# An encoder block on one core: modulation sums ordered one per attention unit, and a later place for the weight chunk's load

## The chip, the cores and the metric

The kernel runs on one core of a Trainium2 chip. The metric is the device time of one launch in microseconds (us). The time before is 1429.08 us, the median of three runs (1422.79 to 1430.99).

## The reference

One layer of an encoder block for one sequence of 1024 tokens with 1024 features, all in float32:

```python
mod = silu(c) @ w_ada + b_ada                    # 6 vectors of 1024
sh_m, sc_m, gt_m, sh_f, sc_f, gt_f = split(mod)
h = rms_norm(x, g_mix) * (1 + sc_m) + sh_m
qa, ka, va, qb, kb, vb = split(h @ w_in)
o_a = neighbourhood_attention(qa, ka, va, rpb)   # 8 heads of 64, an 8 x 16 window
o_b = differential_attention(qb, kb, vb)         # 4 heads, two maps of 64, values of 128
o_b = rms_norm(o_b, subln_w) * (1 - lambda_init)
x = x + gt_m * (concat(o_a, o_b) @ w_out)
h = rms_norm(x, g_ffn) * (1 + sc_f) + sh_f
gate, up = split(h @ w_gate_up)
x = x + gt_f * ((silu(gate) * up) @ w_down)
return rms_norm(x, g_final)
```

A differential head subtracts a multiple of one softmax map from the other. The change touches how four of the six vectors of `mod` are summed (`gt_m`, `sh_f`, `sc_f`, `gt_f`), and when the columns of `w_in` are loaded.

## The kernel before, in words

**Precision.** TensorE multiplies in the type fp32r. Each float32 operand is split into a high part (a copy in fp32r, made by ScalarE) and a low part (the rest, made by VectorE or GpSimd), and each product is three matmuls: high x high, high x low, low x high. So nearly every result that goes back to TensorE gives ScalarE one copy and VectorE one subtraction. In the names, a trailing `h` and `l` are the two parts: `w_h` and `w_l` of a chunk of `w_in`, `pth` and `ptl` (neighbourhood) or `ath` and `atl` (differential) of the transposed probabilities, `vsh` and `vsl` of values. TensorE's lines are all that of a helper, L89, so its rows are told apart by tiles.

**Stages.** From 0 to 66 us the kernel loads `x`, normalizes it and makes the first two modulation vectors. From 66 to 640 us it runs the attention, to 714 us the output projection and the second norm, and to 1421 us the FFN.

**The attention.** A list `seq` has 64 units: 32 of neighbourhood attention, `Na(pr, i)`, four pairs of heads by eight blocks of 128 queries, and then 32 of differential attention, `Da(h, i)`. A unit goes through these steps:
- `score()`: its score matmuls (`ns` and `s` for the two kinds), into two banks for the two heads or maps, alternately; then on VectorE the addition of bias or distance with the row minimum (`np<-ns`, L784; `p<-s`, L682; the minimum is in `nst` or `st`), and on ScalarE the exponential.
- `trans()`: VectorE normalizes (L801 and L803) or combines the two maps (L694 to L697), TensorE transposes (`nt`, `at`), ScalarE copies the high part and VectorE subtracts the low part (L814, L705). These low parts are the last instructions of `trans()`.
- `pv()`, for every second unit: the products with the values, and their addition (`on`, L838 and L839).

The main loop works on the units in a staggered way: in the round of unit n it issues `score()` of n + 1, `pv()` of n - 1, `norm()` of n - 2, `finish()` of n - 3, one step of the modulation sums, and `trans()` of n:

```python
        fill(step * share[1])
        next(mods, None)
...
        u.trans(ats)
```

Between these, `fill()` takes matmuls from a queue of fillers, which give TensorE work while a softmax runs: `gen_qk` (L475) makes the queries or keys of a head from a chunk of `w_in`, in two halves of 24 matmuls (`hf` 0 and 1, tiles `nq`, `nk`, `q`, `k`), `gen_v` (L496) makes values from two chunks in four parts (`ip` 0 to 3, tiles `v0p` to `v3p`), and `gen_mo` makes parts of the output projection (`mo`).

**The chunks of `w_in`.** `next_w()` takes the next chunk, of 128 x 1024, and splits what is still unsplit in the list `loading`; `load_next()` splits what is in `loading` and issues the load of a further chunk (`w_r`, L226) on SyncE's queue. The split is a copy by ScalarE (`w_h`, L201) and a subtraction by GpSimd (`w_l`, L202). One chunk is loaded ahead.

**The modulation sums.** `gen_mods` (L578 to L616) makes a vector `silu(c) @ w` as eight steps for each half of 512 columns: a load of a tile `wm` of 128 x 512 (L587, on GpSimd's queue, up to three under way), and on VectorE `acc = wm * silc[j] + acc` (L596 for the first of the eight, L600 for the others). There are three vectors, so 48 steps, one in each round of the main loop. A further load is issued behind each step. There is a single `acc` tile. After the eighth step the half is finished: for the gate vector, ScalarE and VectorE split `acc` (`gh` L607, `gl` L608), a bias row is loaded (`gb`, L611, SyncE's queue), TensorE adds over the partitions (`gt`) and VectorE adds the bias (`gate_m`, L616); for the others TensorE makes columns (`mvp`) and VectorE adds (`AB`, L210 and L212). A fourth vector, the FFN's gate, is made by the same function in the first group of the FFN, with its loads on SyncE's queue; there the first step of each half is ordered behind an instruction of the second norm, `late_t["done"]`.

**The order.** The program text is not the order of execution. A scheduler sorts the instructions of each engine by a simulated time and the dependencies, and engines then run their own lists strictly in order, waiting for one another by semaphores. `PE.after(x, y)` (L76) adds an order without a wait: `x` stands behind `y` in the schedule. A sum depends only on its `wm` tile and on `acc`, so the scheduler may put it ahead of the round in whose text it stands.

Of the kernel before, what the change touches and what calls it, by code (L numbers as in the profile page):

```python
# [10 lines left out]
F32 = mybir.dt.float32  # L11
# [4 lines left out]
ALU = mybir.AluOpType  # L16
# [3 lines left out]
P = 128  # L20
# [84 lines left out]
def block_kernel(ctx: ExitStack, tc: tile.TileContext, t: dict):  # L105
# [368 lines left out]

    def gen_qk(kind, key, name):  # L475
        w_h, w_l = next_w()
        load_next()
        hd = key[1] + (4 if key[0][0] == "n" else 0)
        slot = qk_t(hd, 0 if kind == "q" else 2)
        mark = G.memset(slot[:, 0:1].bitcast(F32), 0.0)  # L480
        for hf in range(2):
            out = bank(f"{name}_{hf}")
            for k in range(KT):
                sl = slice(k * P, (k + 1) * P)
                hi, lo = hh[k // 2][:, k % 2, :], hl[k // 2][:, k % 2, :]
                for ti, (w, h) in enumerate([(w_h, hi), (w_h, lo), (w_l, hi)]):
                    mm = PE.matmul(out, w[:, sl], h[:, hf * 512:(hf + 1) * 512],
                                   start=(k == 0 and ti == 0), stop=(k == KT - 1 and ti == 2))
                    if mark is not None:
                        PE.after(mm, mark)  # L490
                        mark = None
                yield 0.65
            made = evac_q(out, hd, hf) if kind == "q" else evac_k(out, hd, hf)
        qkv[key] = made

    def gen_v(n, evac):  # L496
        ws = [next_w(), next_w()]
        load_next()
        for ip in range(4):
            out = bank(f"v{n}p{ip}")  # L500
            for ii in range(2):
                i = 2 * ip + ii
                for k in range(KT):
                    w_h, w_l = ws[k // 4]
                    sl = slice((k % 4) * 256, (k % 4 + 1) * 256)
                    hi = hh[k // 2][:, k % 2, i * P:(i + 1) * P]
                    lo = hl[k // 2][:, k % 2, i * P:(i + 1) * P]
                    for ti, (h, w) in enumerate([(hi, w_h), (lo, w_h), (hi, w_l)]):
                        PE.matmul(out[:, ii * 256:(ii + 1) * 256], h, w[:, sl],
                                  start=(k == 0 and ti == 0), stop=(k == KT - 1 and ti == 2))  # L510
                    if k % 2:
                        yield 0.65
            evac(n, ip, out)
        qkv["vd", n] = True

    def v_tiles(n):
# [58 lines left out]
            tb.append(tbh)  # L575
        qkv["tb", pr] = tb

    def gen_mods(steps, raw_of, acc_of, tmp_of, gate, queue, first=None, ahead=2):  # L578

        steps = [(which, n, j) for which in steps for n in range(2) for j in range(KT)]  # L580
        raws = []
# [9 lines left out]
        for at, (which, n, j) in enumerate(steps):  # L591
            load()
            yield
            if j == 0:
                acc = acc_of(f"acc{which}{n}")
                head = V.tensor_scalar(out=acc, in0=raws[at], scalar1=silc[:, 0:1], scalar2=None, op0=ALU.mult)  # L596
                if first is not None:
                    PE.after(head, first)
            else:
                V.scalar_tensor_tensor(out=acc, in0=raws[at], scalar=silc[:, j:j + 1], in1=acc, op0=ALU.mult, op1=ALU.add)  # L600
            if j < KT - 1:
                continue
            if which in (3, 4):
# [14 lines left out]
    queue = []  # L618
# [38 lines left out]
    class Da:  # L657
# [30 lines left out]
        def trans(self, ats):  # L688
# [9 lines left out]
            for b in range(2):  # L698
                tps = bank(f"at{h}_{i}_{b}")
                for j in range(4):  # L700
                    PE.transpose(tps[:, j * P:(j + 1) * P], p[0][:, (4 * b + j) * P:(4 * b + j + 1) * P], ident)
                src = tps.rearrange("p (a b) -> p a b", a=4)
                hi, lo = at_h[b][:, :, e * P:(e + 1) * P], at_l[b][:, :, e * P:(e + 1) * P]
                A.activation(out=hi, in_=src, func=AF.Copy)
                V.tensor_tensor(out=lo, in0=src, in1=hi.bitcast(F32), op=ALU.subtract)  # L705

        def pv(self, ats, pvs):
            h, i = self.h, self.i
# [56 lines left out]
    class Na:  # L765
# [24 lines left out]
        def trans(self, ats):  # L790
# [19 lines left out]
            for m in range(2):  # L810
                src = tps[:, m * 512:m * 512 + nk].rearrange("p (a b) -> p a b", b=P)
                dsl = (slice(None), slice(sl, sl + nk // P), slice(e * P, (e + 1) * P))
                A.activation(out=pt_h[m][dsl], in_=src, func=AF.Copy)
                V.tensor_tensor(out=pt_l[m][dsl], in0=src, in1=pt_h[m][dsl].bitcast(F32), op=ALU.subtract)  # L814

        def pv(self, ats, pvs):
            pr, i = self.pr, self.i
# [49 lines left out]
    def gate_m():  # L867
        if 2 not in gates:
# [1 line left out]
        return gates[2]  # L870

    mods = gen_mods((2, 3, 4), mraw_t, lambda nm: mp.tile([P, 512], F32, tag="acc", bufs=1, name=nm),
                    lambda nm, dt=F32: mp.tile([P, 512], dt, tag="sq", bufs=4, name=nm), gate_m, G)

    oh, ol, wo, x1, late_t = [], [], [[], []], [], {}

    o_at = {}

# [222 lines left out]
    for gi, fs in enumerate(groups):  # L1101
# [27 lines left out]
        if gi == 0:  # L1129
            gtf = gate_t("gate_f")  # L1130
            for _ in gen_mods((5,), lambda nm: lp.tile([P, 512], F32, tag="dt", bufs=4, name=nm),
                              lambda nm: lp.tile([P, 512], F32, tag="macc", bufs=1, name=nm),
                              lambda nm, dt=F32: lp.tile([P, 512], dt, tag="sil", bufs=3, name=nm), lambda: gtf, SY, late_t["done"]):
                pass
        wd = []
        for f in fs:
# [82 lines left out]
```

## Time and profile before

| | us |
|---|---|
| median of three runs | 1429.08 |
| lowest and highest | 1422.79, 1430.99 |
| the profiled execution | 1423.15 |
| its span | 1421.4 |
| TensorE (PE) busy in the span | 1378.5 (97%) |
| VectorE (DVE) busy | 724.2 (51%) |
| ScalarE (ACT) busy | 461.9 (32%) |
| GpSimd (POOL) busy | 291.5 (21%) |

The profile is of one execution; the span is what the trace covers of its time. Busy times are per engine and overlap. SP is the queue of SyncE, which issues most DMAs. The granted clock, PEclk, is the mean TensorE clock of a stretch, where 1.00 is the higher of two levels (2.4 GHz) and 0.50 the lower (1.2 GHz). A busy time of TensorE is modelled from the records of its matmuls, so a long one at the lower clock is busy too.

### The profile page before, as it was taken

The page shows a single profiled execution, that of the slowest core. Times are in us where ns is not written, and L with a number is a line of the kernel's source. Part 1 is how long each engine was busy: PE and PEld are TensorE (multiplying, and loading weights), DVE is VectorE, ACT ScalarE, POOL GpSimd, SP SyncE. Part 2 cuts the span into 40 slices and gives each one's busy share as a digit, 9 for nine tenths or more (in the row PEclk, how much of TensorE's full clock was granted, in tenths as well). Part 3 has the DMA queues.
Part 4 walks back from the last instruction along what each step waited for, and adds up shares of the span by engine and source line. Part 5 has one row for each costly group of instructions (what it writes and reads, how often), then busy time and mean ns, then how long its engine had stood idle before and what let it go on. Part 6 is the DMA issues. An engine that isn't in the chain of part 4 may idle for free.

```text
span 1421.4 us, 17696 instructions
## 1 busy us (share of the span) xinstructions
PE 1378.5 (97%) x7033; PEld 1142.2 (80%) x7033; DVE 724.2 (51%) x1324; ACT 461.9 (32%) x817; POOL 291.5 (21%) x318
## 2 busy tenths in 40 slices
PE   5899998999999999999999999999999999999997
PEld 5698787887898777787888888888888888888886
DVE  5775766748777589656747215113411421151136
ACT  5544444545445365423531220221121012202212
POOL 3021322311112000001430320421221132204201
PEclk8999999999999998999999999999999999999999
DMA  9231514433021251023321210211111121102102
GB/s 371 105 119 49 189 61 129 134 101 114 24 89 60 82 199 53 8 68 112 119 76 43 75 59 1 89 45 45 31 73 45 31 62 57 55 6 89 45 22 96
DMA packets 43826, 114.82 MB, mean 81 GB/s; under 512 B 12723, under 2 KB 12979, under 8 KB 42464
## 3 DMA queue, kind: packets, MB, share of 16 engines
q1 hardware_dynamic: 39280, 99.37, 20.8%
q0 software_dynamic: 4464, 14.33, 3.1%
q8 instruction: 55, 0.90, 0.3%
q14 instruction: 27, 0.22, 0.0%
HBM read 99.26 MB, written 14.42 MB: 80 GB/s over the span
## 4 chain that ended last, share of the span: by engine, by line
PE 90%; DVE 4%; ACT 2%; DMA 1%; issue 1%; POOL 1%; POOLq 0%; DVEq 0%; ACTq 0%
PE gu L89 33%; PE dn L89 17%; PE s L89 5%; PE pv L89 3%; PE mo L89 3%; PE k L89 3%; PE q L89 3%; PE mp L89 3%; PE at L89 2%; PE nk L89 2%; PE npv L89 2%; PE v1p L89 2%; PE v2p L89 2%; PE nq L89 1%; PE v3p L89 1%
## 5 line engine op out<-in xcount | busy, mean ns | idle before, releaser
L1126 DVE TENSOR_TENSOR sg<-sg,gu 128x512 f32<-128x512 f32 x44 | 30.2, 687 | 352.0 <-ACT sg L1125 352.0
L89 PE MATMUL dn<-wd_h,al 128*128 128x512 f32 x352 | 136.9, 389 | 0.0
L89 PE MATMUL dn<-wd_l,ah 128*128 128x512 f32 x352 | 136.9, 389 | 0.0
L89 PE MATMUL dn<-wd_h,ah 128*128 128x512 f32 x352 | 136.9, 389 | 0.0
L1156 DVE TENSOR_TENSOR dt<-dn,gate_f 128x512 f32<-128x512 f32 x96 | 66.4, 691 | 88.1 <-PE dn L89 88.1
L202 POOL TENSOR_TENSOR wg_l<-wg_r,wg_h 128x1024 fp32r<-128x1024 f32 x20 | 48.4, 2420 | 271.9 <-ACT wg_h L201 271.9
L684 ACT ACTIVATE p<-p,st 128x1024 f32<-128x1024 f32 x64 | 73.5, 1148 | 61.7 <-DVE st L682 58.7
L201 ACT ACTIVATE wg_h<-wg_r 128x1024 fp32r<-128x1024 f32 x22 | 23.3, 1060 | 212.2 <-PE dn L89 154.2
L89 PE MATMUL s<-qk 64*128 64x512 f32 x384 | 88.6, 425 | 2.9 <-DVE st L682 2.9
L682 DVE CUSTOM_DVE_ANT_0 p<-s,dist 128x1024 f32<-128x1024 f32 x64 | 77.1, 1218 | 23.7 <-PE s L89 22.8
L202 POOL TENSOR_TENSOR wd_l<-wd_r,wd_h 128x1024 fp32r<-128x1024 f32 x20 | 48.0, 2400 | 163.7 <-ACT wd_h L201 163.7
L89 PEld LDWEIGHTS dn<-wd_h,ah 128*128 128x128 f32 x352 | 66.1, 188 | 13.8
L89 PEld LDWEIGHTS dn<-wd_h,al 128*128 128x128 f32 x352 | 66.1, 188 | 13.7
L89 PEld LDWEIGHTS dn<-wd_l,ah 128*128 128x128 f32 x352 | 66.1, 188 | 13.7
L89 PEld LDWEIGHTS s<-qk 64*128 64x128 f32 x384 | 54.3, 189 | 26.0 <-issue 9.0
L1157 DVE TENSOR_TENSOR x<-x,dt 128x512 f32<-128x512 f32 x96 | 70.0, 729 | 2.9
L1125 ACT ACTIVATE sg<-gu 128x512 f32<-128x512 f32 x44 | 26.0, 590 | 138.4 <-PE gu L89 136.6
L89 PE MATMUL gu<-h2h,wg_h 128*128 128x512 f32 x176 | 68.9, 392 | 0.4 <-DVE sg L1126 0.4
L89 PE MATMUL gu<-h2l,wg_h 128*128 128x512 f32 x176 | 68.7, 391 | 0.0
L89 PE MATMUL gu<-h2h,wu_h 128*128 128x512 f32 x176 | 68.6, 390 | 0.0
L89 PE MATMUL gu<-h2l,wu_h 128*128 128x512 f32 x176 | 68.6, 390 | 0.0
L89 PE MATMUL gu<-h2h,wg_l 128*128 128x512 f32 x176 | 68.5, 389 | 0.0
(308 smaller groups left out, 3467.3 us busy)
## 6 DMA issues: line engine op xcount, KB each, us to landing
w_r<-in_w_in_dram SPq DMA_DIRECT2D x24, 512.0 KB, 3.7
wm<-in_w_ada_l_dram POOLq DMA_DIRECT2D x48, 256.0 KB, 3.5
wg_r<-in_w_gate_up_dram SPq DMA_DIRECT2D x22, 512.0 KB, 3.6
wu_r<-in_w_gate_up_dram SPq DMA_DIRECT2D x22, 512.0 KB, 3.5
wd_r<-in_w_down_dram SPq DMA_DIRECT2D x22, 512.0 KB, 3.5
x<-in_x_dram SPq DMA_DIRECT2D x16, 512.0 KB, 8.5
wada<-in_w_ada_s_dram SPq DMA_DIRECT2D x6, 1024.0 KB, 11.8
v<-vd SPq DMA_DIRECT2D x4, 1024.0 KB, 5.7
```

The lines of the kernel that those rows point to most:

```text
L89: ins = call(*args, **kw)
L201: A.activation(out=hi, in_=raw, func=AF.Copy)
L202: lo_engine().tensor_tensor(out=lo, in0=raw, in1=hi.bitcast(F32), op=ALU.subtract)
L682: V.tensor_tensor_reduce(out=pr, in0=s, in1=dists[0][:, d0:d0 + 1024], scale=1.0, scalar=BIG, op0=ALU.add, op1=ALU.min, accum_out=self.st[ ...
L684: A.activation(out=pr, in_=pr, func=AF.Exp, scale=-1.0, bias=self.st[:, m:m + 1], accum_out=self.st[:, 2 + m:3 + m])
L1125: A.activation(out=sg, in_=gu[:, 0:512], func=AF.Silu)
L1126: V.tensor_tensor(out=sg, in0=sg, in1=gu[:, 512:1024], op=ALU.mult)
L1156: V.tensor_tensor(out=dt_, in0=out, in1=gtf[:, dsl], op=ALU.mult)
L1157: V.tensor_tensor(out=x1[i][:, dsl], in0=x1[i][:, dsl], in1=dt_, op=ALU.add)
```

## The change

First, each step of the modulation sums is ordered behind the instruction that `mark()` names, if there is one. In the attention that is the latest low part written by a `trans()` so far, `late_t["low"]`: since the step stands ahead of `trans()` in the text, it is a low part of the unit before. In the FFN it is `late_t["done"]`, now for every step and not only for the first of eight. Second, `load_next()` moves from the start of a chunk to its middle, behind the first half in `gen_qk`, and behind the second of four parts in `gen_v`. Lines behind the first hunk shift by one to four.

```diff
--- before.py
+++ after.py
@@ -474,7 +474,6 @@
 
     def gen_qk(kind, key, name):
         w_h, w_l = next_w()
-        load_next()
         hd = key[1] + (4 if key[0][0] == "n" else 0)
         slot = qk_t(hd, 0 if kind == "q" else 2)
         mark = G.memset(slot[:, 0:1].bitcast(F32), 0.0)
@@ -491,11 +490,12 @@
                         mark = None
                 yield 0.65
             made = evac_q(out, hd, hf) if kind == "q" else evac_k(out, hd, hf)
+            if hf == 0:
+                load_next()
         qkv[key] = made
 
     def gen_v(n, evac):
         ws = [next_w(), next_w()]
-        load_next()
         for ip in range(4):
             out = bank(f"v{n}p{ip}")
             for ii in range(2):
@@ -511,6 +511,8 @@
                     if k % 2:
                         yield 0.65
             evac(n, ip, out)
+            if ip == 1:
+                load_next()
         qkv["vd", n] = True
 
     def v_tiles(n):
@@ -575,7 +577,9 @@
             tb.append(tbh)
         qkv["tb", pr] = tb
 
-    def gen_mods(steps, raw_of, acc_of, tmp_of, gate, queue, first=None, ahead=2):
+    late_t = {}
+
+    def gen_mods(steps, raw_of, acc_of, tmp_of, gate, queue, mark, ahead=2):
 
         steps = [(which, n, j) for which in steps for n in range(2) for j in range(KT)]
         raws = []
@@ -593,11 +597,11 @@
             yield
             if j == 0:
                 acc = acc_of(f"acc{which}{n}")
-                head = V.tensor_scalar(out=acc, in0=raws[at], scalar1=silc[:, 0:1], scalar2=None, op0=ALU.mult)
-                if first is not None:
-                    PE.after(head, first)
+                step = V.tensor_scalar(out=acc, in0=raws[at], scalar1=silc[:, 0:1], scalar2=None, op0=ALU.mult)
             else:
-                V.scalar_tensor_tensor(out=acc, in0=raws[at], scalar=silc[:, j:j + 1], in1=acc, op0=ALU.mult, op1=ALU.add)
+                step = V.scalar_tensor_tensor(out=acc, in0=raws[at], scalar=silc[:, j:j + 1], in1=acc, op0=ALU.mult, op1=ALU.add)
+            if mark() is not None:
+                PE.after(step, mark())
             if j < KT - 1:
                 continue
             if which in (3, 4):
@@ -702,7 +706,7 @@
                 src = tps.rearrange("p (a b) -> p a b", a=4)
                 hi, lo = at_h[b][:, :, e * P:(e + 1) * P], at_l[b][:, :, e * P:(e + 1) * P]
                 A.activation(out=hi, in_=src, func=AF.Copy)
-                V.tensor_tensor(out=lo, in0=src, in1=hi.bitcast(F32), op=ALU.subtract)
+                late_t["low"] = V.tensor_tensor(out=lo, in0=src, in1=hi.bitcast(F32), op=ALU.subtract)
 
         def pv(self, ats, pvs):
             h, i = self.h, self.i
@@ -811,7 +815,7 @@
                 src = tps[:, m * 512:m * 512 + nk].rearrange("p (a b) -> p a b", b=P)
                 dsl = (slice(None), slice(sl, sl + nk // P), slice(e * P, (e + 1) * P))
                 A.activation(out=pt_h[m][dsl], in_=src, func=AF.Copy)
-                V.tensor_tensor(out=pt_l[m][dsl], in0=src, in1=pt_h[m][dsl].bitcast(F32), op=ALU.subtract)
+                late_t["low"] = V.tensor_tensor(out=pt_l[m][dsl], in0=src, in1=pt_h[m][dsl].bitcast(F32), op=ALU.subtract)
 
         def pv(self, ats, pvs):
             pr, i = self.pr, self.i
@@ -870,9 +874,9 @@
         return gates[2]
 
     mods = gen_mods((2, 3, 4), mraw_t, lambda nm: mp.tile([P, 512], F32, tag="acc", bufs=1, name=nm),
-                    lambda nm, dt=F32: mp.tile([P, 512], dt, tag="sq", bufs=4, name=nm), gate_m, G)
-
-    oh, ol, wo, x1, late_t = [], [], [[], []], [], {}
+                    lambda nm, dt=F32: mp.tile([P, 512], dt, tag="sq", bufs=4, name=nm), gate_m, G, lambda: late_t.get("low"))
+
+    oh, ol, wo, x1 = [], [], [[], []], []
 
     o_at = {}
 
@@ -1130,7 +1134,7 @@
             gtf = gate_t("gate_f")
             for _ in gen_mods((5,), lambda nm: lp.tile([P, 512], F32, tag="dt", bufs=4, name=nm),
                               lambda nm: lp.tile([P, 512], F32, tag="macc", bufs=1, name=nm),
-                              lambda nm, dt=F32: lp.tile([P, 512], dt, tag="sil", bufs=3, name=nm), lambda: gtf, SY, late_t["done"]):
+                              lambda nm, dt=F32: lp.tile([P, 512], dt, tag="sil", bufs=3, name=nm), lambda: gtf, SY, lambda: late_t["done"]):
                 pass
         wd = []
         for f in fs:
```

VectorE, neighbourhood attention, second pair of heads (`np_2` is its third unit). Before, from the last `ptl` of unit 0 on:

```order
L814 TENSOR_TENSOR ptl_0_1_1542<-nt_0_1550,pth_0_1_1540 128x2x128
L616 TENSOR_TENSOR gate_m<-gt_1532,gb_1530 128x512
L600 SCALAR_TENSOR_TENSOR acc_1632<-wm_1537,silc,acc_1632 128x512
L600 SCALAR_TENSOR_TENSOR acc_1632<-wm_1634,silc,acc_1632 128x512
L784 ISA np_2_1591,nst_2_1590<-ns_2_1589,tb_1424 128x384
L784 ISA nst_2_1590 128x1
L784 ISA np_2_1591,nst_2_1590<-ns_2_1589,tb_1428 128x384
L784 ISA nst_2_1590 128x1
L600 SCALAR_TENSOR_TENSOR acc_1632<-wm_1709,silc,acc_1632 128x512
```

With the change:

```order
L818 TENSOR_TENSOR ptl_0_1_1542<-nt_0_1550,pth_0_1_1540 128x2x128
L600 TENSOR_SCALAR acc_1630<-wm_1340,silc 128x512
L620 TENSOR_TENSOR gate_m<-gt_1532,gb_1530 128x512
L788 ISA np_2_1591,nst_2_1590<-ns_2_1589,tb_1424 128x384
L788 ISA nst_2_1590 128x1
L788 ISA np_2_1591,nst_2_1590<-ns_2_1589,tb_1428 128x384
L788 ISA nst_2_1590 128x1
L788 ISA np_3_1662,nst_3_1661<-ns_3_1660,tb_1424 128x384
L788 ISA nst_3_1661 128x1
```

The first sum of a new vector (`acc_1632`, now `acc_1630`) is now behind `ptl_0_1`, no other follows, and `np_2` and `np_3` come next.

VectorE at the change to the third pair of heads (`np_0`, `np_1`, with new tables). Before:

```order
L596 TENSOR_SCALAR acc_2183<-wm_1979,silc 128x512
L814 TENSOR_TENSOR ptl_3_0_1983<-nt_7_2033,pth_3_0_1981 128x2x128
L814 TENSOR_TENSOR ptl_3_1_1984<-nt_6_1992,pth_3_1_1982 128x3x128
L600 SCALAR_TENSOR_TENSOR acc_2183<-wm_2028,silc,acc_2183 128x512
L814 TENSOR_TENSOR ptl_3_1_1984<-nt_7_2033,pth_3_1_1982 128x2x128
L616 TENSOR_TENSOR gate_m<-gt_2132,gb_2130 128x512
L600 SCALAR_TENSOR_TENSOR acc_2183<-wm_2136,silc,acc_2183 128x512
L461 SCALAR_TENSOR_TENSOR qk_2009<-nq_1_2074,qk_2009 128x512
L600 SCALAR_TENSOR_TENSOR acc_2183<-wm_2185,silc,acc_2183 128x512
L600 SCALAR_TENSOR_TENSOR acc_2183<-wm_2258,silc,acc_2183 128x512
L784 ISA np_0_2052,nst_0_2051<-ns_0_2050,tb_2042 128x256
L784 ISA nst_0_2051 128x1
```

With the change:

```order
L602 SCALAR_TENSOR_TENSOR acc_1630<-wm_1864,silc,acc_1630 128x512
L818 TENSOR_TENSOR ptl_3_1_1984<-nt_7_2031,pth_3_1_1982 128x2x128
L602 SCALAR_TENSOR_TENSOR acc_1630<-wm_1923,silc,acc_1630 128x512
L461 SCALAR_TENSOR_TENSOR qk_2007<-nq_1_2074,qk_2007 128x512
L788 ISA np_0_2050,nst_0_2049<-ns_0_2048,tb_2040 128x256
L788 ISA nst_0_2049 128x1
L788 ISA np_0_2050,nst_0_2049<-ns_0_2048,tb_2044 128x256
L788 ISA nst_0_2049 128x1
L612 TENSOR_TENSOR gl_2127<-acc_1630,gh_2126 128x512
L788 ISA np_1_2080,nst_1_2079<-ns_1_2078,tb_2040 128x384
L788 ISA nst_1_2079 128x1
```

Here the new vector's sums (`acc_2183`) stood ahead of `np_0`; now the old vector's last ones (`acc_1630`) stand there, and the split of it (`gl`) behind `np_0`. In the order before, two more of the new vector's sums stand between `np_1` and `np_2`; in the order now its first one stands behind `np_2`.

TensorE, differential attention, last head, scores of its seventh unit (`s_6_0` and `s_6_1` are the two maps). Before:

```order
L89 MATMUL mo_0_5777<-ext,oh_5326 128x512
L89 MATMUL mo_0_5777<-ext,ol_5327 128x512
L89 MATMUL mo_0_5777<-ext,oh_5326 128x512
L89 MATMUL s_6_1_5849<-qk_4703 128x512 x6
L89 MATMUL s_7_0_5926<-qk_4703 128x512 x6
L89 MATMUL mo_1_5840<-ext,oh_5326 128x512
```

With the change:

```order
L89 MATMUL mo_0_5777<-ext,ol_5327 128x512
L89 MATMUL mo_0_5777<-ext,oh_5326 128x512
L89 MATMUL s_6_0_5848<-qk_4701 128x512
L89 MATMUL s_6_1_5849<-qk_4701 128x512
L89 MATMUL s_6_0_5848<-qk_4701 128x512
L89 MATMUL s_6_1_5849<-qk_4701 128x512
```

Before, `s_6_0` had stood some 35 rows earlier, alone; now the two maps' matmuls alternate, six of each.

On GpSimd the `wm` loads, which stood in groups of two to eight, stand one or two at a time. On SyncE, a `w_r` that stood ahead of the four loads of `v_1` (L553) stands behind them.

## Rows read from the trace of the kernel before

**Rows 1.** The page, part 4: the chain that ended last, by engine.

```profile
PE 90%; DVE 4%; ACT 2%; DMA 1%; issue 1%; POOL 1%; POOLq 0%; DVEq 0%; ACTq 0%
```

**Rows 2.** Windows: stretch; length, then busy PE, PEld, DVE, ACT, POOL; PEclk, DMA, GB/s.

```profile
150.00:204.00 54.00, 51.67 (x291) 42.49 (x291) 37.14 (x85) 22.42 (x53) 17.86 (x32) 0.97 0.44 140
204.00:262.00 58.00, 52.58 (x347) 44.75 (x346) 41.76 (x107) 27.32 (x70) 15.08 (x42) 0.94 0.32 104
262.00:282.00 20.00, 18.57 (x148) 16.45 (x148) 16.82 (x45) 10.62 (x27) 8.47 (x19) 1.00 0.51 154
320.00:362.00 42.00, 39.45 (x185) 29.70 (x185) 33.74 (x63) 19.73 (x34) 6.70 (x9) 0.92 0.28 96
412.00:520.00 108.00, 108.00 (x622) 85.95 (x621) 73.95 (x135) 49.74 (x83) 13.05 (x8) 1.00 0.21 73
520.00:556.00 36.00, 35.51 (x168) 27.64 (x168) 34.83 (x63) 23.12 (x39) 1.01 (x1) 0.81 0.52 194
```

**Rows 3.** Waits of TensorE, whole span: waiter, releaser, us in total, times, longest.

```profile
PE nt L89 <- DVE nst L784: 3.9, 1, 3.9
PE s L89 <- DVE st L682: 2.9, 3, 1.4
PE ns L89 <- DVE nst L784: 2.3, 1, 2.3
PE npv L89 <- DVE ptl L814: 1.5, 2, 1.4
```

**Rows 4.** Timeline of VectorE: start, us, engine, line, what, [idle before, releaser].

```profile
155.12 0.69 DVE L616 TENSOR_TENSOR gate_m<-gt,gb 128x512 f32<-128x512 f32 x1 [0.99 <-DMA gb<-in_rows_dram]
155.73 3.40 DVE L600 SCALAR_TENSOR_TENSOR acc<-wm,silc,acc 128x512 f32<-128x512 f32 x2
160.00 2.92 DVE L600 SCALAR_TENSOR_TENSOR acc<-wm,silc,acc 128x512 f32<-128x512 f32 x1
209.66 2.96 DVE L600 SCALAR_TENSOR_TENSOR acc<-wm,silc,acc 128x512 f32<-128x512 f32 x1
278.27 1.94 DVE L600 SCALAR_TENSOR_TENSOR acc<-wm,silc,acc 128x512 f32<-128x512 f32 x1 [0.45 <-DMA wm<-in_w_ada_l_dram]
328.96 1.28 DVE L697 SCALAR_TENSOR_TENSOR p<-p,st,p 128x1024 f32<-128x1024 f32 x1
```

**Rows 5.** Timeline of TensorE: two waits, and nq at two clocks.

```profile
160.14 0.97 PE L89 MATMUL ns<-qk 64*128 64x384 f32 x6 [2.33 <-DVE nst L784]
161.63 0.63 PE L89 MATMUL nq<-hh,w_h 128*128 128x512 f32 x1
164.34 0.40 PE L89 MATMUL nq<-hl,w_h 128*128 128x512 f32 x1
329.10 1.66 PE L89 MATMUL s<-qk 64*128 64x512 f32 x6 [1.35 <-DVE st L682]
```

**Rows 6.** The tile acc: line, engine, duration in ns (min/median/max).

```profile
L600 DVE SCALAR_TENSOR_TENSOR acc<-wm,silc,acc x56: 731/750/2964, 74.7 to 750.5; 128x512 f32<-128x512 f32 x56
```

**Rows 7.** Timeline of GpSimd: two of its subtractions.

```profile
155.41 2.38 POOL L202 TENSOR_TENSOR w_l<-w_r,w_h 128x1024 fp32r<-128x1024 f32 x1 [0.78 <-ACT w_h L201]
209.67 2.40 POOL L202 TENSOR_TENSOR w_l<-w_r,w_h 128x1024 fp32r<-128x1024 f32 x1
```

**Rows 8.** Timeline of TensorE: score matmuls of one map, and of both.

```profile
337.68 1.65 PE L89 MATMUL s<-qk 64*128 64x512 f32 x6
392.08 1.65 PE L89 MATMUL s<-qk 64*128 64x512 f32 x12
```

**Rows 9.** Waits of GpSimd from 60 to 540 us.

```profile
POOL w_l L202 <- ACT w_h L201: 55.4, 11, 17.2
```

**Rows 10.** A weight chunk: its load's issue, its split, and loads to landing.

```profile
212.09 0.33 SPq L226 DMA_DIRECT2D w_r<-in_w_in_dram  x1
235.04 1.06 ACT L201 ACTIVATE w_h<-w_r 128x1024 fp32r<-128x1024 f32 x1 [0.26 <-PE nk L89]
DMA to landing us min/median/max: 3.3/3.6/5.8
```


## The prediction

> **What bounds the kernel now.** I read four views, in this order. The chain of waits: TensorE carries 90% of it, VectorE 4% [rows 1]. So the change can gain only where TensorE idles, runs at a lower clock, or does the same matmuls in less time. The table by stage shows where that is: the FFN behind 781 us has nothing to do with the attention's sums, and only a few stretches of the attention show TensorE busy for less than their length, or a granted clock under 1.00 [rows 2]. The waits say on whom: on `nst` (3.9 and 2.3 us) and three times on `st` (2.9 us), results of VectorE's softmax operations, and 1.5 us on `ptl`, its low part [rows 3]. The time rows show what VectorE did meanwhile: at 155.73 two modulation sums took 3.40 us ahead of the `np` for whose `nst` TensorE stood until 160.14, and at 209.66 one sum took 2.96 us [rows 4, 5].
>
> Two things stand in these rows. First, the sums come in bursts: a vector's eight run as soon as the one `acc` tile is free. Second, a sum that takes 0.750 us at the median takes up to 2.964 [rows 6] when it meets the GpSimd subtraction `w_l`: the sums at 155.73, 160.00, 209.66 and 278.27 each lie beside a `w_l` of 2.4 us that began within about a microsecond of them; two are shown [rows 4, 7]. The Trainium skill, "SBUF — State Buffer", on the shared port pair, says that a VectorE instruction with two SBUF inputs and a GpSimd one that reads SBUF exclude each other for a whole instruction; the stretched sums agree.
>
> The clock is the other half. After the wait that ended at 160.14 the `nq` matmuls take 0.63 us each, and 0.40 from 164.34 on [rows 5]: the lower of the two levels for some 3 us. Its price in a stretch is (1 − granted clock) × length, from rows 2.
>
> **The change, part by part.** A measurement of this kernel can tell about 0.5%, 7.1 us, from no change. The sum is made against the profiled execution, 1423.15 us (span 1421.4), which lies 5.9 below the median of the three timed runs, 1429.08; the forecast is the difference, put to that median.
>
> *The bursts at 150 to 204 us.* Ahead of `np_2` VectorE ran a vector's first four sums; in the new order only the first. The three that go took 0.75 + 3.40 = 4.15 us [rows 4, 6], more than TensorE's idle 54.00 − 51.67 = 2.33 us [rows 2], so all of that goes, and with it the clock's 0.03 × 54 = 1.6 us. Term: **3.9 us**. Late next is `gate_m`, which still stands ahead of `np_2` and waits 0.99 us for its bias [rows 4]; it ended by 155.8, and TensorE ran out only at 160.14 − 2.3 = 157.8, so 2 us of cover are left.
>
> *The bursts at 204 to 262 us.* Ahead of the `np_2` for which TensorE waited 3.9 us [rows 3], VectorE ran a vector's first sum and six more, one of them of 2.96 us and five of 0.75: 6.7 us beside the first. The new order has three sums of the old vector there, 2.25 us, and the first of the new one behind `np_2`. It is some 4.5 us shorter, against 58.00 − 52.58 = 5.4 us idle and 0.06 × 58 = 3.5 us of clock [rows 2]. A ScalarE chain lies there too (the exponentials between `np` and the normalization), so I take 3.5 of the idle and 2.5 of the clock: **6.0**, bounds 3 and 8.9.
>
> *262 to 282 us.* The wait for `ptl` behind the sum at 278.27, which took 1.94 us [rows 3, 4]; with one sum per unit its load has a unit's time. The idle 20.00 − 18.57 [rows 2] goes: **1.4**.
>
> *320 to 362 us.* Idle 2.55 us, clock 0.08 × 42 = 3.4 [rows 2]. Three sums, some 2.2 us, ahead of the `p` that TensorE waits for until 329.10 go, but the combination of the two maps, 1.28 us [rows 4, 5], moves ahead of it. The second wait there has no sum just in front of it. Bounds 0 and 5.9; I take **2.0**, since only the first wait is of the kind that is changed.
>
> *Score matmuls.* They use 64 rows of the array. Six in a row took 1.65 us, and twelve, of both maps in turn, 1.65 too [rows 8]: the two halves ran side by side. A unit wholly in turn has 11 places where a matmul of one map stands next to one of the other, worth 1.65 / 11 = 0.15 us each. The order has 101 such places before and 143 with the change; 23 of the 42 lie in two units where VectorE sets the pace (34.83 busy of 36 us at 520 to 556 [rows 2]), so I count 19 × 0.15 = **2.8**, bounds 0 and 6.3.
>
> *What it adds.* Some 16 sums now stand in units of differential attention, one behind each unit's last low part; in the order before these were two bursts of eight. At 0.750 us [rows 6] they cost nothing where VectorE has room (73.95 of 108 us busy at 412 to 520 [rows 2]), and 0.75 each where it has not. I charge **2.0**, one new wait like that at 329.10 with some clock; bounds 0 and 12.
>
> *Loads of the sums.* Each `wm` load on GpSimd's queue now waits for a sum of its unit, and stands ahead of a `w_l`, of blanking writes, or of the power for the head norm. GpSimd already waits 55.4 us for `w_h` ahead of its `w_l` [rows 9], so a load in front is covered: 0. If that cover goes, a `w_l` that comes late by its own 2.4 us [rows 7] stops the next chunk once. A gain hangs on it too: with a `w_l` behind a load that a sum has just released, the next sum is a unit away and the two hardly meet; it is part of the first three terms and isn't added again.
>
> *The later load of the weight chunk.* I expect **0**. `load_next()` splits only what is in `loading`, and `next_w()` has emptied that just before, in the old place as in the new: nothing is split in the middle, and what moves is the issue of a chunk's load. On ScalarE `w_h` stands where it stood; on SyncE a `w_r` falls behind four `v` loads at one place. That `w_r` was issued at 212.09 and its split began at 235.04, 19 us more than the 3.6 us to landing [rows 10]. Bounds: 0, and a loss of 3.6 us if all that cover were gone.
>
> *The FFN's gate sums* are all tied to the event to which the first of them was tied: 0.
>
> Sum: 3.9 + 6.0 + 1.4 + 2.0 + 2.8 − 2.0 = 14.1 us. 1423.15 − 14.1 = 1409.0 in the profile's terms, and 1429.08 − 14.1 = **1415** for the median.
>
> **The rivals.** *The next wait takes over* (0.17). Once the sums are out of the way, `np` waits for ScalarE's exponentials, or the clock falls at another place. For it: at 204 to 262 both chains are there, and the second wait at 320 to 362 has no sum in it. Against it: 412 to 520, without bursts in it, is wholly busy at 1.00 [rows 2]. Then a third remains, about −5: 1424.
>
> *Sums that meet another subtraction* (0.07). There are as many `w_l` as before, and the combination of the two maps also has two SBUF inputs. If the four collisions, (3.40 − 1.50) + (2.92 − 0.75) + (2.96 − 0.75) + (1.94 − 0.75) = 7.5 us above the median [rows 4, 6], come back at other places, half of the gain goes: 14.1 − 7.5 = 6.6, 1422.5. By the rule of the Trainium skill named above, whichever starts second is held for the whole of the other; the order does not say which that will be.
>
> *VectorE becomes the bound in the differential units* (0.11). A sum now stands between a unit's last low part and the `p` of the next, and cannot be put off. Where VectorE has no room just then, TensorE waits for `st` as at 329.10 [rows 5], and the clock may fall, 3.4 us for two such waits at 320 to 362, 1.7 each. It decides where VectorE is busy above some 85%: 33.74 of 42 us there is 80% [rows 2], and a sum more per 9 us makes 88%. Such waits at 10 of the 16 units cost 10 × (0.75 + 1.7) = 24; less the early terms, 3.9 + 6.0 + 1.4 + 2.8, that is +10: 1439.
>
> *The forecast* has 0.65.
>
> **How the numbers follow.** Faster by over 7.1 us: the forecast and a part of the first two rivals, 0.71. Within: most of these two, 0.18. Slower: the third, 0.11. The lower end takes all idle and clock terms (3.9 + 8.9 + 1.4 + 5.9) and all pairs (6.3): −26, 1403. The upper end takes in the first two rivals and leaves out the third: 1428.
>
> **What would show it.** Right: single `acc` rows a unit apart, none above 1 us; no wait of `ns` or `nt` above 1 us at 150 to 262 and a granted clock of 0.98 or more there; twelve `s` matmuls in one group in more units; `w_r`, `w_h` and `w_l` where they were. Wrong: `acc` among what releases `p`, TensorE waiting for `st` in many differential units, VectorE above 85% from 362 to 520, or a weight load of TensorE waiting for `w_l`.

## The result, and the profile after

The changed kernel takes 1410.62 us (median of 4 runs, 1408.87 to 1417.70), the kernel before 1428.37 us in the same comparison (4 runs). The medians lie 17.75 us apart. The ratio over all these runs, which is not the quotient of the medians, is 0.9892 with a 95% interval from 0.9863 to 0.9922: faster by 15.4 us (11 to 20). The profiled execution took 1409.25 us, its span is 1407.4, 14.0 us less than before.

The first five stretches of [rows 2] in the changed kernel, by windows (the columns are the same; what is in a window has moved up by as much as 19 us):

```profile
150.00:204.00 54.00, 54.00 (x317) 45.10 (x316) 34.95 (x93) 25.53 (x62) 17.77 (x36) 1.00 0.45 135
204.00:262.00 58.00, 55.88 (x403) 48.67 (x402) 47.32 (x129) 30.30 (x81) 16.60 (x46) 1.00 0.39 121
262.00:282.00 20.00, 20.00 (x128) 17.06 (x128) 15.26 (x39) 10.98 (x26) 8.51 (x14) 1.00 0.60 201
320.00:362.00 42.00, 41.62 (x219) 31.47 (x218) 32.90 (x64) 21.17 (x37) 5.95 (x9) 1.00 0.13 44
412.00:520.00 108.00, 103.85 (x566) 81.51 (x565) 79.57 (x141) 53.36 (x90) 14.35 (x11) 0.95 0.33 115
```

Up to 362 us TensorE is busy nearly throughout, at the full clock. From 412 to 520, where it had been wholly busy, it now idles for 4.15 us and the clock is 0.95.

TensorE's waits in the attention (60 to 640 us; a wait of `bc`, 1.6 us, is the same in both kernels and left out), which answer to [rows 3], and the sums' own row, which answers to [rows 6]:

```profile
PE s L89 <- DVE st L686: 3.0, 3, 1.5
PE k L89 <- DVE qk L461: 2.3, 1, 2.3
PE at L89 <- DVE p L701: 1.5, 1, 1.5
PE nt L89 <- DVE nst L788: 1.4, 1, 1.4
```

```profile
L602 DVE SCALAR_TENSOR_TENSOR acc<-wm,silc,acc x56: 736/744/2566, 99.7 to 735.2; 128x512 f32<-128x512 f32 x56
```

The wait of `ns` (2.3 us) is gone, that of `nt` is down from 3.9 to 1.4, that of `npv` for `ptl` is gone. Waits of `k` and `at` are new. The three waits for `st` take as much as before, but lie elsewhere: 0.4 us of them ahead of 420 us, where it had been 2.5. The longest sum, 2.57 us at 228.40, meets a `w_l`, but no wait of TensorE comes of it.

Where the time went is read best at fixed points of the program. TensorE's timeline has them: the first matmul of a neighbourhood pair's first or third value product (`npv`), the first transposes of a differential unit (`at`, the 5th, 14th and 15th unit), and the FFN's first matmul. Before:

```profile
127.61 0.28 PE L89 MATMUL npv<-pth,v 128*128 128x256 f32 x1
167.56 0.28 PE L89 MATMUL npv<-pth,v 128*128 128x256 f32 x1
246.99 0.28 PE L89 MATMUL npv<-pth,v 128*128 128x256 f32 x1
301.33 0.28 PE L89 MATMUL npv<-pth,v 128*128 128x256 f32 x1
368.96 0.82 PE L89 MATMUL at<-ident,p 128*128 128x128 f32 x6
453.74 0.66 PE L89 MATMUL at<-ident,p 128*128 128x128 f32 x4
463.48 0.60 PE L89 MATMUL at<-ident,p 128*128 128x128 f32 x4
678.19 0.48 PE L89 MATMUL gu<-h2h,wg_h 128*128 128x512 f32 x1
```

After:

```profile
128.56 0.28 PE L89 MATMUL npv<-pth,v 128*128 128x256 f32 x1
164.52 0.28 PE L89 MATMUL npv<-pth,v 128*128 128x256 f32 x1
237.77 0.28 PE L89 MATMUL npv<-pth,v 128*128 128x256 f32 x1
289.36 0.28 PE L89 MATMUL npv<-pth,v 128*128 128x256 f32 x1
349.97 0.60 PE L89 MATMUL at<-ident,p 128*128 128x128 f32 x4
438.59 1.07 PE L89 MATMUL at<-ident,p 128*128 128x128 f32 x8
453.76 0.60 PE L89 MATMUL at<-ident,p 128*128 128x128 f32 x4
664.79 0.48 PE L89 MATMUL gu<-h2h,wg_h 128*128 128x512 f32 x1
```

The differences are +0.95, −3.04, −9.22, −11.97, −18.99, −15.15, −9.72 and −13.40 us. So 19.9 us are gained from the first point to the fifth, and 5.6 of them are lost again in the differential units. The start's 0.95 was there ahead of all that was changed: the last `mp` matmul begins at 65.5 us before and at 66.4 after. The FFN has the same length.

Two points do not always enclose the same work, since fillers can move across them. The windows from the fourth point to the fifth, before and after, show it:

```profile
301.33:368.96 67.63, 65.08 (x328) 50.63 (x327) 47.63 (x95) 29.59 (x55) 10.18 (x15) 0.95 0.25 82
289.36:349.97 60.61, 60.23 (x320) 46.79 (x319) 45.18 (x93) 28.05 (x55) 11.35 (x14) 1.00 0.28 90
```

Eight matmuls fewer lie between them, and from the fifth point to the last there are 12 more (1754 instead of 1742). At TensorE's mean of 0.18 us for a matmul there (307.14 us busy with 1742) that is an estimated 2 us, by which the gain ahead of the fifth point and the loss behind it both look too large.

The largest single loss is between the 14th and the 15th unit: 9.74 us before, 15.17 after, with 62 matmuls in either. There the changed kernel's TensorE, VectorE and GpSimd show:

```profile
435.51 2.23 PE L89 MATMUL s<-qk 64*128 64x512 f32 x12
441.97 0.79 PE L89 MATMUL k<-hh,w_h 128*128 128x512 f32 x1 [2.31 <-DVE qk L461]
446.83 0.63 PE L89 MATMUL k<-hh,w_l 128*128 128x512 f32 x1
448.61 0.40 PE L89 MATMUL k<-hl,w_h 128*128 128x512 f32 x1
```

```profile
437.93 2.25 DVE L602 SCALAR_TENSOR_TENSOR acc<-wm,silc,acc 128x512 f32<-128x512 f32 x1
440.10 1.21 DVE L686 CUSTOM_DVE_ANT_0 p<-s,dist 128x1024 f32<-128x1024 f32 x1
441.24 0.68 DVE L461 SCALAR_TENSOR_TENSOR qk<-q,qk 128x512 fp32r<-128x512 f32 x1
```

```profile
437.17 2.46 POOL L202 TENSOR_TENSOR w_l<-w_r,w_h 128x1024 fp32r<-128x1024 f32 x1 [6.72 <-ACT w_h L201]
```

One sum, on its own, meets a `w_l` (437.17 to 439.63) and takes 2.25 us instead of 0.74; behind it wait a `p` and the `qk` that frees the bank for the `k` matmuls. TensorE stands for 2.31 us, and then runs its `k` matmuls at the lower clock until about 448 (0.63 us each, and 0.40 from there on; the granted clock of the whole stretch is 0.77). The Trainium skill, "SBUF — State Buffer", on the shared port pair, has the one that starts second wait for the whole of the other. The trace agrees roughly: the sum starts 0.76 us behind `w_l` and ends 0.55 us behind it, a little less than the 0.74 us that a sum takes alone.

### The profile page after: what moved, and what is told of

Same layout as the page of the kernel before. It is cut to its first block, busy times and chain, and to the rows that moved or that the text cites. A ratio compares the mean times of both kernels' runs of the same rounds, so it can differ in the third digit from the quotient of the medians.

```text
span 1407.4 us, 17670 instructions
## 1 busy us (share of the span) xinstructions
PE 1368.0 (97%) x7033; PEld 1135.0 (81%) x7033; DVE 720.4 (51%) x1324; ACT 460.9 (33%) x817; POOL 291.5 (21%) x318
## 4 chain that ended last, share of the span: by engine, by line
PE 93%; DVE 3%; DMA 1%; ACT 1%; issue 1%; POOL 1%; SPq 0%; DVEq 0%; POOLq 0%; ACTq 0%
PE gu L89 34%; PE dn L89 17%; PE s L89 5%; PE mo L89 3%; PE k L89 3%; PE pv L89 3%; PE q L89 3%; PE mp L89 3%; PE nk L89 2%; PE npv L89 2%; PE sps L89 2%; PE at L89 2%; PE v1p L89 2%; PE v0p L89 2%; PE v3p L89 2%; PE v2p L89 2%
## 5 line engine op out<-in xcount | busy, mean ns | idle before, releaser
L1160 DVE TENSOR_TENSOR dt<-dn,gate_f 128x512 f32<-128x512 f32 x96 | 66.4, 691 | 88.1 <-PE dn L89 88.1
L89 PE MATMUL s<-qk 64*128 64x512 f32 x384 | 81.9, 420 | 3.0 <-DVE st L686 3.0
L89 PEld LDWEIGHTS s<-qk 64*128 64x128 f32 x384 | 49.8, 186 | 24.5 <-issue 10.6
L591 POOL DMA_DIRECT2D wm<-in_w_ada_l_dram x48 | 27.4, 571 | 202.2 <-DVE acc L602 100.7
```

The source lines that it names most:

```text
L89: ins = call(*args, **kw)
L591: queue.dma_start(out=raws[-1], in_=t["w_ada_l"][which - 2, n, :, j, :])
L1160: V.tensor_tensor(out=dt_, in0=out, in1=gtf[:, dsl], op=ALU.mult)
```

## The experiments

All ratios are against the kernel before, on the same chip. The runs were made on several chips, so runs of different groups are compared by their ratios first.

**The two parts apart.** `e1_marks` is the changed kernel with `load_next()` where it was; `e2_load` is the kernel before with only `load_next()` moved.

```diff
 def gen_qk(kind, key, name):
     w_h, w_l = next_w()
+    load_next()
...
-            if hf == 0:
-                load_next()
```

> The change without its second part: the sums are ordered behind the low parts, and the weight chunk's load stands where it stood before. Theory (the sums' order brings it all): the time of the changed kernel within noise, about 14 us below the kernel before, ratio 0.989 to 0.991. Rival (the later load brings a part, by moving loads out of the way of the sums'): 3 to 6 us of the gain are missing, ratio 0.993 to 0.995.

> The second part alone: the chunk's load in the middle of the present chunk, the sums as before. Theory: nothing is split later, so the kernel before within noise, ratio 0.998 to 1.002, with the waits for nst at 160 and 222 us still there. Rival: the moved load brings 3 to 6 us, ratio 0.996 or less.

Measured: 0.9899 (0.9875 to 0.9923) and 1.0006 (0.9991 to 1.0021). The sums' order brings all of it, the later load nothing that can be measured; in `e2_load` both waits for `nst`, 3.9 and 2.3 us, are still there.

**The marks in one kind of unit.** `e3_na` keeps `late_t["low"]` in the neighbourhood units only, `e4_da` in the differential units only.

```diff
-                late_t["low"] = V.tensor_tensor(out=lo, in0=src, in1=hi.bitcast(F32), op=ALU.subtract)
+                V.tensor_tensor(out=lo, in0=src, in1=hi.bitcast(F32), op=ALU.subtract)
```

> The change with the marks only in the neighbourhood units; in the differential units the sums are free to come in bursts as before. Theory (the early waits are the sums' bursts, and the differential half brings pairs of score matmuls but as much in new waits): about 12 us gained up to 300 us, and little change behind it, -10 to -13 us in all, ratio 0.991 to 0.993. Rival (the differential half is a pure loss, as the sums there hold up VectorE): faster than the changed kernel, -17 us or more, ratio 0.988 or less.

> The change with the marks only in the differential units; in the neighbourhood units the bursts are as before. Theory: the waits at 160 and 222 us stay, and of the differential half 0 to -4 us are left (pairs gained less new waits), ratio 0.997 to 1.000. Rival (a pure loss there): +3 to +6 us, ratio 1.002 to 1.004.

Measured: 0.9863 (0.9844 to 0.9883), that is 1407.30 us, and 1.0014 (0.9993 to 1.0036). The marks in the neighbourhood units are the whole gain. Those in the differential units bring none. `e3_na` misses its theory and lies in its rival's range: each of its five runs (1405.32 to 1407.90 us) is faster than each of the six of `e1_marks` and the four of the changed kernel (1407.93 at the least). By the ratios the marks there cost 4 to 5 us. `e4_da` gives 2 us; it lies between its theory's range and its rival's, and its interval does not tell it from no change. Where the gain of `e3_na` lies, the same fixed points tell:

```profile
291.64 0.28 PE L89 MATMUL npv<-pth,v 128*128 128x256 f32 x1
352.84 0.60 PE L89 MATMUL at<-ident,p 128*128 128x128 f32 x4
663.32 0.48 PE L89 MATMUL gu<-h2h,wg_h 128*128 128x512 f32 x1
```

−9.69 at the first, −16.12 at the second, −14.87 at the last. Between the first two, `e3_na` gains 6.4 us with its differential sums in bursts, nearly the 7.0 of the changed kernel, but not in the same way (14 matmuls fewer than before lie between the points, 314 instead of 328). Before, TensorE waited for `st` twice there: 1.35 us at 329.10, with a burst in front [rows 5], and 1.20 us at 347.07, among the scores of the fifth unit. What is left, first in `e3_na` and then in the changed kernel:

```profile
318.52 1.67 PE L89 MATMUL s<-qk 64*128 64x512 f32 x6 [1.23 <-DVE st L686]
327.47 1.66 PE L89 MATMUL s<-qk 64*128 64x512 f32 x6 [0.38 <-DVE st L686]
```

With the burst the first wait stays (318.52), and the second is gone. Without the burst the first is gone, and 0.38 us of waiting are left in the fifth unit. So the first wait came from the burst there; the second did not.

**Meeting, or number?** `e7_no_meet` is the kernel before without the GpSimd subtraction of the chunks of `w_in`.

```diff
+        if lo_eng == [G] and name[1:].isdigit():
+            A.activation(out=hi, in_=raw, func=AF.Copy)
+            G.memset(lo.bitcast(F32), 0.0)
+            return hi, lo
         return split_into(raw, hi, lo)
```

> The kernel before, bursts and all, in which GpSimd writes zeros into each w_l of the chunks of w_in instead of the subtraction (the low part of these weights is left out), so that no sum has a GpSimd instruction that reads the same memory beside it. Theory A (it was the meeting of sums and w_l that made the waits): no sum above 1 us, and the waits at 160 and 222 us shrink by the 1.9 to 4.4 us that the stretched sums took too much, to 0 and under 2; -5 to -8 us in all. Theory B (it was the number of sums in front, whatever each takes): the waits stay within 1 us of 2.3 and 3.9, and the time within 3 us of the kernel before.

Measured: 0.9936 (0.9918 to 0.9953), 9 us faster. The sums' row, a wait of TensorE, and two rows of VectorE:

```profile
L604 DVE SCALAR_TENSOR_TENSOR acc<-wm,silc,acc x56: 730/751/754, 75.6 to 748.2; 128x512 f32<-128x512 f32 x56
```

```profile
217.24 0.69 PE L89 MATMUL nt<-ident,np 128*128 128x128 f32 x2 [4.01 <-DVE np L807]
```

```profile
210.65 0.75 DVE L604 SCALAR_TENSOR_TENSOR acc<-wm,silc,acc 128x512 f32<-128x512 f32 x1 [2.10 <-DMA wm<-in_w_ada_l_dram]
216.17 0.75 DVE L604 SCALAR_TENSOR_TENSOR acc<-wm,silc,acc 128x512 f32<-128x512 f32 x1 [1.40 <-DMA wm<-in_w_ada_l_dram]
```

No sum is above 0.754 us, so it was the meeting that stretched them. How much of TensorE's waits the stretching made, this run does not settle, because the scheduler made other lists for it.

The wait of 2.3 us near 160 is gone. But the `nst` of `np_2`, with five sums in front instead of four, comes only 0.8 us earlier (159.3 instead of 160.1), and `ns`, which had stood behind two `nq` matmuls and waited for it, now stands behind 21 of them:

```profile
162.94 0.79 PE L89 MATMUL ns<-qk 64*128 64x384 f32 x6
```

Behind two (the third starts at 158.5) it would still have waited, by estimate, 0.8 us. The rows of the kernel before point the same way: 1.9 of the 2.33 us are the stretch, 3.40 instead of 1.50 us [rows 4].

The 4.01 us near 220 are not the wait that was there before. They are a wait for `np` one place earlier in TensorE's list, where it had been 0.45 us; the wait for `nst`, which had been 3.86, is down to 0.68. TensorE is idle for 4.7 us at the two places instead of 4.3, although no sum is stretched. The cause is one that neither theory named: a burst goes at the pace of its loads. A sum at the head of VectorE's list that has to wait for its `wm` tile holds VectorE idle, 2.10 and 1.40 us here, with `np` behind it. In the kernel before no sum from 204 to 262 us waited for its load; the stretched one took the time instead. Each of the two is enough to hold up `np`. The 9 us are a little more than theory A had, and three times theory B's bound.

**Only the head of each burst held.** In `e8_head` the mark binds the first of eight sums alone.

```diff
-            if mark() is not None:
+            if j == 0 and mark() is not None:
                 PE.after(step, mark())
```

> The changed kernel, but of each eight sums only the first is ordered behind a low part; the other seven may follow in a burst. Theory (a burst hurts by where it begins and by its length): the first sum goes where it is in the changed kernel, two to four follow ahead of the next np, and about half of the gain is lost, ratio 0.993 to 0.997. Rival (only the place of the first counts, since a burst behind a low part falls into VectorE's idle time): the changed kernel within 3 us, ratio 0.987 to 0.991.

Measured: 1.0015 (1.0001 to 1.0029). Not half of the gain is lost, as expected, but all of it:

```profile
PE npv L89 <- DVE ptl L818: 4.8, 1, 4.8
PE nt L89 <- DVE nst L788: 3.9, 2, 2.8
PE ns L89 <- DVE nst L788: 2.3, 1, 2.3
```

```profile
L602 DVE SCALAR_TENSOR_TENSOR acc<-wm,silc,acc x56: 724/751/3207, 95.2 to 755.2; 128x512 f32<-128x512 f32 x56
```

The bursts begin later and meet `w_l` again (3.2 us at the most). What counts is that the sums are apart, not where the first one stands.

**The meeting in the changed kernel.** `e10_after_no_meet` puts the edit of `e7_no_meet` into the changed kernel.

> The changed kernel in which GpSimd writes zeros into each w_l of the chunks of w_in instead of the subtraction (the low part of these weights is left out). Theory A (what the differential half costs is one place, where a sum met a w_l, took 2.25 us and held up the k matmuls for 2.3 us with 2.6 us of clock behind it): the sum takes 0.75 us, that wait falls under 1 us, 3 to 6 us faster than the changed kernel, ratio 0.985 to 0.987. Theory B (the place of the sums there costs, not their length): the wait of k stays above 1.5 us and the time is within 2 us of the changed kernel's, ratio 0.988 to 0.990.

Measured: 0.9868 (0.9841 to 0.9896), 1409.23 us, and no wait of `k` in its profile; no sum takes more than 0.754 us. In `e1_marks`, `e4_da` and `e11_two_sums`, as in the changed kernel, the same sum takes 2.25 or 2.26 us and `k` waits for 2.3 to 3.0; here neither is there. That speaks for the meeting as the cause. It does not prove it, since VectorE's list is another one too (`qk` stands right behind the sum, and no longer behind a `p`); by the changed kernel's rows the stretch is 2.25 − 0.74 = 1.51 of the 2.31 us. The price is not shown: the run is 3.4 us faster than the changed kernel by the ratios, in theory A's range, 1.4 by the medians, and the intervals overlap. The stretch between the 14th and the 15th unit is 12.77 us here, 2.4 less than in the changed kernel, with 75 matmuls in it instead of 62 and a granted clock of 1.00 instead of 0.77.

```profile
432.62 0.64 PE L89 MATMUL at<-ident,p 128*128 128x128 f32 x4
445.39 0.60 PE L89 MATMUL at<-ident,p 128*128 128x128 f32 x4
```

**Has VectorE room?** `e11_two_sums` adds 16 instructions to the last vector, behind its sums.

```diff
+            if which == 4:
+                V.scalar_tensor_tensor(out=acc, in0=raws[at], scalar=0.0, in1=acc, op0=ALU.mult, op1=ALU.add)
```

> The changed kernel with a second instruction of the same size behind each of the 16 sums of the last vector (it adds nothing, its factor is 0). Theory A (VectorE has room in the differential units): 0 to 5 us more than the changed kernel, ratio 0.989 to 0.993. Theory B (VectorE sets the pace there, each 0.75 us counts): 16 x 0.75 = 12 us more and some clock, ratio 0.997 to 1.005.

Measured: 0.9883 (0.9851 to 0.9915), 1411.30 us: not to be told from the changed kernel, and slightly under theory A's range, while theory B's 12 us are ruled out. VectorE has room in the differential units; its share of the time is not what costs there.

**The price of alternation.** In `e5_after_pairs`, `e6_before_pairs` and `e9_na_pairs` each score matmul of a differential unit is ordered behind the one before it in the text (in the changed kernel, the kernel before, and `e3_na`).

```diff
+            for x, y in zip(mm, mm[1:]):
+                PE.after(y, x)
```

> The changed kernel with the score matmuls of a differential unit held in the order of the text, so that the two maps' matmuls alternate in nearly all units (some 328 places instead of 143). Theory A (alternation is worth 0.15 us a place, and what stands in its way is only the schedule): some 185 places more, up to -28 us, ratio 0.970 to 0.980. Theory B (TensorE must then wait until both banks for the scores are free, where before it ran the first map early): new waits for st of about a microsecond in most units eat it, -5 to +10 us, ratio 0.986 to 0.997 against the kernel before.

> The kernel before with the score matmuls of a differential unit held in alternation (some 330 places instead of 95). Theory A (a place is worth 0.05 us net, as in the run with the changed kernel, whatever the sums do): 235 x 0.05 = 9 to 12 us faster, ratio 0.991 to 0.994. Theory B (with bursts of sums in the way, VectorE frees the two banks later, and TensorE, which can no longer run the first map early, waits longer): within 4 us of the kernel before, ratio 0.997 to 1.003.

> Marks in the neighbourhood units alone (the fastest so far) and alternating score matmuls as in the run beside it. Theory A: 0.15 us x 225 places, some -30 us on top of -20, ratio 0.965 to 0.975. Theory B: between the marks in the neighbourhood units alone and 10 us more, ratio 0.985 to 0.994.

Measured: 0.9817 (0.9790 to 0.9844), 0.9868 (0.9841 to 0.9894) and 0.9811 (0.9796 to 0.9826). None of the three lies in the range of either of its theories. The groups of score matmuls from 60 to 640 us (busy, mean ns | idle before), of the kernel before, of `e6_before_pairs`, of the changed kernel and of `e5_after_pairs`:

```profile
L89 PE MATMUL s<-qk 64*128 64x512 f32 x384 | 88.6, 425 | 2.9 <-DVE st L682 2.9
```

```profile
L89 PE MATMUL s<-qk 64*128 64x512 f32 x384 | 66.8, 436 | 8.4 <-DVE st L687 8.4
```

```profile
L89 PE MATMUL s<-qk 64*128 64x512 f32 x384 | 81.9, 420 | 3.0 <-DVE st L686 3.0
```

```profile
L89 PE MATMUL s<-qk 64*128 64x512 f32 x384 | 67.2, 433 | 8.6 <-DVE st L691 8.6
```

Both theories hold a part: the matmuls take 21.8 us less in the kernel before and 14.7 less in the changed one, and 5.5 or 5.6 us of new waits for `st` take a part back. In all it is 18.8 us for 235 places, 0.08 each, and 9 (by the medians) to 11 us (by the ratios) for 185 places, 0.05 to 0.06 each, on top of the change: the two gains do not add up. (The 95 places of the kernel before are those within a unit; the prediction's 101 count six between two units as well.) With the marks in the neighbourhood units and alternation, the median is 1400.73 us, 27 below the kernel before; with all marks and alternation it is 1401.91. Both are faster than the changed kernel; between them the runs don't decide.

## Why the prediction was right

The forecast was 14.1 us below the kernel before; 15.4 were measured, and 14.0 between the two profiled executions. The first two terms are right in size and by their own mechanism. That the rest fits too is luck: by the fixed points the next two terms were too low, by 1.4 and 5.0 us, and the last two, 2.8 − 2.0 = 0.8 in sum, too high by 6.4.

- **The bursts at 150 to 204 us: 3.9 predicted.** From the first fixed point to the second 4.0 us were gained; idle time and loss of clock are both gone. The place of the sums was the cause; how much of it was their number and how much the meeting with `w_l`, `e7_no_meet` does not settle.
- **The bursts at 204 to 262 us: 6.0.** 6.2 us between the second and the third point; TensorE's idle time in the stretch is down from 5.4 to 2.1 us, and the loss of clock is gone. The count of VectorE's time in front of `np_2` was right in size. `e7_no_meet` adds that it isn't the stretched sum alone: without it the sums wait for their loads. A wait of `nt` for `nst` of 1.4 us is left, at 216.61; the prediction's sign of being right was none above 1 us.
- **262 to 282 us: 1.4.** 2.75 us between the third and the fourth point, which lie further apart than the stretch. The idle 1.43 is gone; what the rest is was not tested.
- **320 to 362 us: 2.0, with bounds to 5.9.** 7.0 us up to the fifth point. The step that failed is "only the first wait is of the kind that is changed". The first wait went, but the second also fell, from 1.20 to 0.38 us; idle is down from 2.55 to 0.38 us and the clock up from 0.92 to 1.00, 2.2 + 3.4 = 5.6 us, near the upper bound. The eight matmuls fewer between the points are, by estimate, the rest. In `e3_na`, where the burst and the first wait are still there, the second is gone too, so what removed the second was something ahead of it, and not the sums beside it. Which instruction it is was not tested.
- **Score matmuls: 2.8.** The price was read from a row that isn't typical: twelve in 1.65 us [rows 8]. In the changed kernel the twelve at 435.51 took 2.23, which makes (3.30 − 2.23) / 11 = 0.10 us a place, and the runs above show 0.05 to 0.08 net. So 19 places were worth 1 to 1.5 us.
- **What it adds: 2.0, bounds 0 and 12.** 5.6 us are lost from the fifth point to the last, with the gain of alternation already in it and some 2 us of work that had stood ahead of the fifth point; the marks in the differential units cost 2 to 5 us by whole runs. A single place like the one that was charged exists, at 441.97, but it is a wait of `k` and not of `s`, and more than twice as dear as the term: 2.31 us of waiting and some 13 matmuls that start 0.20 us further apart, 4.9 us. The third rival's mechanism fell (`e11_two_sums`): it isn't VectorE's share, which is 71% from 362 to 520 us. The second rival's came true in part: two sums meet a `w_l`, at 228.40 and 437.93, where before four did, so the sign "none above 1 us" failed. The first of the two costs TensorE nothing; the second, on its own and a unit away from the others, costs what was just told.
- **The later load: 0.** `e2_load` shows it.
- The chance of a gain above 7.1 us was put at 0.71, and the measured time is inside the range, a little below the middle.

## What to carry to other kernels

Work that is off the critical path does harm in bursts: spread it to one piece per round, behind the last instruction of a round that others wait for. Try that in each kind of round by itself: here it brought the whole gain in one kind and cost something in the other. Count in front of a waiting instruction not only the busy time of what was moved there, but also what that work itself waits for, since an engine's list stands still behind it. Holding only the first piece of a burst is not spreading it.

## What the runs showed that was not expected

Two executions of nearly the same order differ most in a single place. `e1_marks` and the changed kernel have the same waits of TensorE from 100 to 490 us, and their profiled executions differ by 8.7 us of span. By windows, first the changed kernel, then `e1_marks`:

```profile
520.00:545.00 25.00, 21.56 (x114) 16.51 (x113) 24.63 (x48) 14.08 (x24) 1.01 (x1) 0.93 0.28 96
545.00:570.00 25.00, 25.00 (x137) 19.30 (x137) 15.71 (x31) 9.02 (x15) 1.01 (x1) 1.00 0.00 1
```

```profile
520.00:545.00 25.00, 23.96 (x93) 18.50 (x91) 19.69 (x36) 11.60 (x19) 1.01 (x1) 0.64 0.24 71
545.00:570.00 25.00, 24.57 (x118) 19.38 (x119) 14.85 (x30) 8.65 (x15) 1.01 (x1) 0.87 0.00 1
```

From 520 to 545 us, where VectorE is busy for 24.63 of 25 us in the changed kernel and for 19.69 in `e1_marks`, the granted clock was 0.93 in one execution and 0.64 in the other: (0.29 + 0.13 of the next) × 25 = 10.5 us, of which 2.0 come back because TensorE idles less. That is nearly all of the 8.7. Runs of the changed kernel alone scatter by nearly 9 us; whether this place makes that scatter too is not shown, as there is one profile of each kernel. A difference of one or two per mille between two such kernels can't be read from one profile.

The Trainium skill, "TensorEngine Tiling (Array Packing)", theoretical speedup, allows up to twice for a contraction of 64 or less. With 330 of 352 places in alternation the score matmuls took 66.8 us instead of 88.6, 1.33 times as fast, from a start with 95 places.
